# The second norm's first two channel tiles, multiplied before the token root is known

## The chip, the cores and the metric

The kernel runs on one core of one Trainium2 chip. The time is the device time of one execution in microseconds. A core has TensorE (PE in the profile; its weight loads are PEld), VectorE (DVE), ScalarE (ACT), GpSimd (POOL) and SyncE (SP, which here issues DMAs). Each engine takes its own instructions in order and waits at semaphores for the others.

## The reference

One hybrid backbone block over 512 latent tokens of width 2048, with a prefix of 256 context tokens: adaLN norm, two groups of recurrent heads, gates, an output projection with a gated residual, then the part that matters here:

```
x  = x + gt1 * (y @ w_out)
h2 = rmsnorm(x, g_norm2) * (1 + sc2) + sh2        # rmsnorm: x * rsqrt(mean(x*x) + 1e-6) * g, per token
u_gate, u_val = split(h2 @ w_up)                  # 2048 -> 2 x 5504
g  = conv3x3_depthwise(u_gate, 8 x 64 grid) + conv_b
x  = x + gt2 * ((silu(g) * u_val) @ w_down)
return rmsnorm(x, g_final)
```

With s = g_norm2 (1 + sc2) per channel, b = sh2 per channel and r the root per token, a product of h2 with w_up is r * ((s x) @ w_up) + (b @ w_up): the root is one factor for each token, and the shift gives one number for each output channel.

## The kernel before, in words

Activations lie transposed: 16 channel tiles x2[k] of 128 channels (partitions) by 512 tokens. Every matrix product is made in three: an operand is split into a rounded high part and a low part (the remainder), and high by high, high by low and low by high are added in a PSUM bank (`mm3`, L111; its matmuls are recorded at L98). A split is a cast on ScalarE (L90) and a subtraction on VectorE (L91).

The output projection runs in four units wo0 to wo3. Each has four accumulators of 128 channels and goes through the 16 input tiles in eight pairs; a pair loads 128x1024 weights by DMA (`load_split`, tile raw), splits them (hi, lo; two buffers each) and issues 4 x 2 x 3 matmuls of 512 columns. At a unit's end four channel tiles of x2 are updated (L1057) and squared on ScalarE (L1065). The squares of the first twelve tiles are added on VectorE to one tile; the last four tiles' squares stay apart, so five sums are left.

`token_rstd` (L1068) adds each of the five sums over the channels with a matmul by a column of ones: four matmuls of one output column for each, in two passes each, 40 records in all (ps_rms, L1077). A root follows in small steps on ScalarE and VectorE (L159 to L171), and four matmuls spread the root over all partitions (rb_rms, L1088).

The scaling loop (L1137) then goes through the 16 tiles: VectorE multiplies by the root (L84), ScalarE makes the high operand by scale and bias (L1143, tile b), VectorE scales and shifts x2 itself (L1144) and subtracts for the low operand (L81). Tiles 0 to 7 have operands by halves of 256 tokens, tiles 8 to 15 of 512.

`up_two(0)` and `up_two(1)` (L1199) are the first two units of the MLP's up projection, each with four blocks of 128 output channels (two for the gate branch, two for the value branch), eight pairs of channel tiles each; the bank of a gate block is copied to a padded image (L1213), of a value block to val or stage (L1215). Between them `token_sums` builds sums and differences over token halves for a seven-product scheme, which all later blocks (`up_seven`, f = 4 to 42) use, each with its convolution and its share of the down projection. At the end comes a last norm.

A scheduler sets the order of instructions on each engine by priority; `tc.high_priority()` raises it, `tc.keep_in_program_order` pins an instruction to the order in which the code is written, and `tc.issue_after` puts one behind a named other. Tiles come from pools. The pools of the norm (rp among them, which holds the squares and the root) are closed after the root, and the pools fp, tp and bp (the b operands) take their space; the first use of a new tile waits for the last use of what lay there. PSUM has six banks for accumulators and two for small sums.

Of the kernel before, what the change touches and what calls it, by code (L numbers as in the profile page):

```python
# [11 lines left out]
F32 = mybir.dt.float32  # L12
F32R = mybir.dt.float32r
# [5 lines left out]
P = 128  # L19
D = 2048  # L20
# [50 lines left out]
def block_kernel(ctx: ExitStack, tc: tile.TileContext, a: dict, out: bass.AP):  # L71
# [121 lines left out]
    third, turn = [None], [0]  # L193
# [8 lines left out]
    def load_split(src, name, n=2, w=512):  # L202
# [3 lines left out]
        nc.sync.dma_start(raw, src)  # L206
        with tc.high_priority():
            ins = split(hi, lo, raw)
# [862 lines left out]
    def token_rstd(sums, pl, name, n=T, twice=False):  # L1071

        nj = n // P
        ps = psb(f"ps_{name}", (P, nj))
        for i, sq in enumerate(sums):
            for j in range(nj):
                PE.matmul(ps[:, j : j + 1], sq[:, P * j : P * j + P], cst[:, C_ONE : C_ONE + 1],  # L1077
                          start=(i == 0 and j == 0), stop=(i == len(sums) - 1), skip_group_check=True)
        var, scr, r = (pl.tile([P, nj], F32, name=f"{t}_{name}", tag=t) for t in ("rs1", "rs2", "rs3"))
        root(r, ps, D, scr, var)  # L1080
# [6 lines left out]
        for j in range(nj):  # L1087
            PE.matmul(o[:, P * j : P * j + P], r[:, j : j + 1].to_broadcast([P, P]), ident, start=True, stop=True)  # L1088
# [4 lines left out]
    sums2 = []  # L1093
    for n in range(4):
        accs = unit(a["w_out"][n], f"wo{n}", yh, yl)
        with tc.high_priority():
# [4 lines left out]
            for i in range(4):  # L1101
                square(4 * n + i, sums2, rp, "sq")
    with tc.high_priority():
        r2 = token_rstd(sums2, rp, "rms2")
# [30 lines left out]

    with tc.high_priority():
        for k in range(KT):  # L1137
            t = x2[k]
            sk, bk = modc[4][:, k : k + 1], modc[3][:, k : k + 1]
            for sl in (slice(0, TH), slice(TH, T)) if k == 0 else (slice(0, T),):  # L1140
                mul(t[:, sl], t[:, sl], r2[:, sl])
            for sl, (h, l) in halves(k):
                S.activation(h, t[:, sl], AF.Identity, scale=sk, bias=bk)  # L1143
            V.tensor_scalar(out=t, in0=t, scalar1=sk, scalar2=bk, op0=ALU.mult, op1=ALU.add)  # L1144
            for sl, (h, l) in halves(k):
                sub(l, t[:, sl], h.bitcast(F32))
# [31 lines left out]
    stage = [fp.tile([P, T], F32, name=f"stage{i}") for i in range(2)]  # L1178
# [20 lines left out]
    def up_two(n):  # L1199

        accs = [acc(f"u{n}_{i}") for i in range(4)]
        for kp in range(KP):
            wh, wl = load_split(a["w_up0"][n, kp], f"u{n}_{kp}")
            for i, o in enumerate(accs):
                for kk in range(2):
                    k = 2 * kp + kk
                    for sl, (h, l) in halves(k):
                        mm3(o[:, sl], wh[:, kk, P * i : P * i + P], wl[:, kk, P * i : P * i + P],
                            h, l, k == 0 and sl.start == 0, k == KT - 1, skip_group_check=True)
        vals = []  # L1210
        with tc.high_priority():
# [260 lines left out]
```

## Time and profile before

| | |
|---|---|
| median of three runs | 2482.74 us (2481.16 to 2483.55) |
| the profiled execution | 2482.2 us, its span 2480.1 us, mean granted clock 0.993 |
| TensorE busy | 2441.8 us, 98% of the span |
| VectorE, ScalarE, GpSimd busy | 1746.8, 1117.9, 370.4 us |
| output projection's last wide product starts | 1131.64 us |
| first product of the first up unit starts | 1139.15 us |
| first and second up unit end | 1231.97 us |

Rows of the profile give, in this order, a start or a line, the busy time, the engine, the operation with its result and its operands, the shape, and the count of records; a bracket gives the idle time of the engine ahead of the row and what ended it. A matmul's record reaches past the start of the next one, so its cost in a row of equal ones is the distance of the starts. Matmuls with full-precision operands leave two records each.

### The profile page before, as it was taken

What the parts mean: (1) busy time and instruction counts of PE and PEld (TensorE: products, weight loads), DVE (VectorE), ACT (ScalarE), POOL (GpSimd) and SP (SyncE); (2) the same over time, 40 slices, a digit from 0 to 9 for tenths busy, and PEclk for the clock granted to TensorE, in tenths of its full rate; (3) what the DMA queues carried; (4) which work ended last, traced back from release to release, by engine and by line L of the source; (5) the groups of instructions that cost most, each with busy time, mean ns of one, the idle gap of its engine ahead of it and who ended that gap; (6) DMA issues with size and microseconds to landing.
All of it is one profiled execution on the core that took longest, in us unless ns stands there. A gap on an engine that the chain in (4) does not pass through costs nothing.

```text
span 2480.1 us, 35194 instructions
## 1 busy us (share of the span) xinstructions
PE 2441.8 (98%) x13594; PEld 2105.6 (85%) x13594; DVE 1746.8 (70%) x2464; ACT 1117.9 (45%) x1660; POOL 370.4 (15%) x362
## 2 busy tenths in 40 slices
PE   7999999999999999999999999999999999999998
PEld 4888899988988888888888888888888888888887
DVE  5566766554455678867887777777777777777884
ACT  4224544322213444434555555555555555555553
POOL 0000000000000344440011111111111111111101
PEclk9999999999999999999999999999999999999999
DMA  9751112124342778862488888888888888888762
GB/s 374 275 188 52 35 43 77 60 85 136 122 142 94 266 261 297 278 208 95 139 188 192 189 193 190 193 196 191 193 192 189 189 192 189 193 190 190 179 207 68
DMA packets 137911, 429.66 MB, mean 173 GB/s; under 512 B 15504, under 2 KB 19984, under 8 KB 137744
## 3 DMA queue, kind: packets, MB, share of 16 engines
q1 hardware_dynamic: 104688, 348.24, 42.8%
q0 software_dynamic: 31968, 78.66, 20.3%
q8 instruction: 106, 1.74, 0.3%
q10 hardware_dynamic: 1088, 0.52, 0.1%
q14 instruction: 61, 0.50, 0.1%
HBM read 381.22 MB, written 46.14 MB: 172 GB/s over the span
## 4 chain that ended last, share of the span: by engine, by line
PE 91%; issue 3%; DVE 2%; DMA 1%; ACT 0%; POOL 0%; SPq 0%; POOLq 0%; DVEq 0%; ACTq 0%
PE a L98 18%; PE x L98 18%; PE dn L98 16%; PE v L98 9%; PE wo L98 7%; PE ga L98 7%; PE w L98 4%; PE po L98 4%; PE u L98 4%; PE ps_m L98 1%; PE sl L98 1%; PE cst L98 1%; PE s L98 1%; PE mc L325 1%; DMA xl<-in_xT 0%
## 5 line engine op out<-in xcount | busy, mean ns | idle before, releaser
L91 DVE TENSOR_TENSOR lo_q<-q,hi_q 128x1024 fp32r<-128x1024 f32 x195 | 235.4, 1223 | 142.4 <-ACT spare L1323 117.6
L90 ACT CAST hi_q<-q 128x1024 fp32r<-128x1024 f32 x195 | 205.1, 1052 | 229.7 <-PE dn L98 161.9
L98 PE MATMUL dn<-gh,lo_d 128*128 128x512 f32 x660 | 257.2, 390 | 0.0
L98 PE MATMUL dn<-gl,hi_d 128*128 128x512 f32 x660 | 257.2, 390 | 0.0
L98 PE MATMUL dn<-gh,hi_d 128*128 128x512 f32 x660 | 257.1, 390 | 0.0
L1190 DVE SCALAR_TENSOR_TENSOR cv<-pad,cwt,cv 128x512 f32<-128x512 f32 x328 | 246.2, 751 | 6.3 <-ACT cv L1188 0.5
L98 PE MATMUL x<-bt,hi_q 128*128 128x512 f32 x936 | 235.3, 393 | 0.0
L98 PEld LDWEIGHTS x<-bt,hi_q 128*128 128x128 f32 x936 | 167.4, 188 | 30.8
L1231 POOL DMA_DIRECT2D spare<-in_w_up x78 | 68.8, 883 | 731.2 <-DMA spare<-in_w_up 650.2
L314 POOL TENSOR_TENSOR sumg_m<-sumg_m,raw_m 128x512 f32<-128x512 f32 x74 | 124.1, 1677 | 199.4 <-ACT raw_m L313 112.0
L98 PE MATMUL a<-hi_h,hTh 128*128 128x256 f32 x512 | 150.1, 293 | 0.0
L91 DVE TENSOR_TENSOR lo_d<-raw_d,hi_d 128x1024 fp32r<-128x1024 f32 x84 | 101.3, 1206 | 65.9 <-ACT hi_d L90 51.5
L306 DVE SCALAR_TENSOR_TENSOR sum_m<-raw_m,csil,sum_m 128x512 f32<-128x512 f32 x112 | 145.4, 1299 | 1.3
L98 PEld LDWEIGHTS dn<-gl,hi_d 128*128 128x128 f32 x660 | 123.9, 188 | 26.3 <-DVE gl L91 0.2
L98 PEld LDWEIGHTS dn<-gh,hi_d 128*128 128x128 f32 x660 | 123.8, 188 | 26.4 <-ACT gh L90 0.3
L98 PEld LDWEIGHTS dn<-gh,lo_d 128*128 128x128 f32 x660 | 123.9, 188 | 26.2
L98 PE MATMUL a<-lo_h,hTh 128*128 128x256 f32 x512 | 144.7, 283 | 0.0
L98 PE MATMUL a<-hi_h,hTl 128*128 128x256 f32 x512 | 144.7, 283 | 0.0
L91 DVE TENSOR_TENSOR lo_q<-spare,hi_q 128x1024 fp32r<-128x1024 f32 x78 | 95.3, 1222 | 56.7 <-ACT hi_q L90 56.7
L98 PEld LDWEIGHTS x<-bt,lo_q 128*128 128x128 f32 x936 | 125.6, 188 | 10.4 <-ACT u L1297 1.1
L90 ACT CAST hi_h<-raw_h 128x1024 fp32r<-128x1024 f32 x64 | 67.0, 1047 | 138.8 <-PE a L98 131.2
L98 PE MATMUL x<-bt,lo_q 128*128 128x256 f32 x936 | 128.2, 279 | 0.7 <-ACT u L1297 0.7
(366 smaller groups left out, 5864.2 us busy)
## 6 DMA issues: line engine op xcount, KB each, us to landing
raw_m<-in_w_mod SPq DMA_DIRECT2D x192, 512.0 KB, 5.0
q<-in_w_up SPq DMA_DIRECT2D x117, 512.0 KB, 4.5
raw_d<-in_w_down SPq DMA_DIRECT2D x81, 512.0 KB, 3.7
spare<-in_w_up SPq DMA_DIRECT2D x78, 512.0 KB, 4.6
spare<-in_w_up POOLq DMA_DIRECT2D x78, 512.0 KB, 7.4
raw_h<-in_w_heads SPq DMA_DIRECT2D x64, 512.0 KB, 3.5
x2d<-stage POOLq DMA_DIRECT2D x72, 256.0 KB, 5.1
x2d<-spare POOLq DMA_DIRECT2D x72, 256.0 KB, 5.1
```

What stands on the lines that cost most here:

```text
L90: split_ins[0] = S.copy(hi, x).ins
L91: return V.tensor_tensor(out=lo, in0=x, in1=hi.bitcast(F32), op=ALU.subtract).ins
L98: ins = PE.matmul(*args, **kw)
L306: V.scalar_tensor_tensor(out=parts["v"], in0=raw[:, 0, :], scalar=ce, in1=parts["v"], op0=ALU.mult, op1=ALU.add)
L314: G.tensor_tensor(out=parts["g"], in0=parts["g"], in1=raw[:, 1, :], op=ALU.add)
L325: tc.keep_in_program_order(PE.matmul(ps[:, i : i + 1], po[:, P * i : P * i + P], cst[:, C_ONE : C_ONE + 1], start=True, stop=True))
L1190: V.scalar_tensor_tensor(out=t3, in0=src, scalar=w, in1=t3, op0=ALU.mult, op1=ALU.add)
L1231: eng.dma_start(q, a["w_up"][f - FIRST, i, j].rearrange("p k c -> p (k c)"), **kw)
```

## The change

Channel tiles 0 and 1 are multiplied by the norm's scale alone, without the root, and split (unh, unl), while the second output unit still runs. Their products with the first pair of weights of the first up unit (u0_0) go to four accumulators un0 to un3 (`plain_product`), without waiting for the root. TensorE's order is pinned here: blocks 0 and 1, all the sums of squares, block 2, the broadcast, the shift's columns, block 3. The shift's share of these two tiles is a full-precision product of the unsplit weights with the shift column (`shift_column`). VectorE later multiplies the four accumulators by the root (r2s, a copy of the broadcast) into the images and value tiles, and when the unit is done adds its result and the shift's column to them, in place of the four copies. The first up unit starts at its second pair. Tiles 2 and 3 are scaled first and as before; from tile 4 on ScalarE applies scale and bias in place and casts, and VectorE's scale-and-shift falls away. Tiles 0 and 1 are scaled last; the second up unit and the token sums use them. The loads of two pairs are put behind named instructions.

```diff
--- before.py
+++ after.py
@@ -190,7 +190,7 @@
             for f in now:
                 f()
 
-    third, turn = [None], [0]
+    third, turn, last_raw = [None], [0], [None]
 
     def hi_tile(name, n):
 
@@ -204,6 +204,7 @@
         hi = hi_tile(f"hi_{name}", n * w).rearrange("p (n w) -> p n w", n=n)
         lo = wlo.tile([P, n, w], F32R, name=f"lo_{name}", tag="lo")
         nc.sync.dma_start(raw, src)
+        last_raw[0] = raw
         with tc.high_priority():
             ins = split(hi, lo, raw)
         run_later((split_ins[0], ins))
@@ -1068,16 +1069,17 @@
         else:
             add(sums[0], sums[0], sq)
 
-    def token_rstd(sums, pl, name, n=T, twice=False):
+    def token_rstd(sums, pl, name, n=T, twice=False, ps=None, between=lambda: None):
 
         nj = n // P
-        ps = psb(f"ps_{name}", (P, nj))
+        ps = ps or psb(f"ps_{name}", (P, nj))
         for i, sq in enumerate(sums):
             for j in range(nj):
-                PE.matmul(ps[:, j : j + 1], sq[:, P * j : P * j + P], cst[:, C_ONE : C_ONE + 1],
-                          start=(i == 0 and j == 0), stop=(i == len(sums) - 1), skip_group_check=True)
+                mm(ps[:, j : j + 1], sq[:, P * j : P * j + P], cst[:, C_ONE : C_ONE + 1],
+                   start=(i == 0 and j == 0), stop=(i == len(sums) - 1), skip_group_check=True)
         var, scr, r = (pl.tile([P, nj], F32, name=f"{t}_{name}", tag=t) for t in ("rs1", "rs2", "rs3"))
-        root(r, ps, D, scr, var)
+        root(r, ps[:, 0:nj], D, scr, var)
+        between()
         if twice:
             oo = [psb(f"rb_{name}{i}", (P, n)) for i in range(2)]
             for o in oo:
@@ -1085,12 +1087,12 @@
             return oo
         o = psb(f"rb_{name}", (P, n))
         for j in range(nj):
-            PE.matmul(o[:, P * j : P * j + P], r[:, j : j + 1].to_broadcast([P, P]), ident, start=True, stop=True)
+            mm(o[:, P * j : P * j + P], r[:, j : j + 1].to_broadcast([P, P]), ident, start=True, stop=True)
         return o
 
     dr = pool(ctx, "dr", 1, bass.MemoryType.DRAM)
     x2d = [dr.tile([P, T], F32, name=f"x2d{k}", tag=f"x2d{k}") for k in range(KT)]
-    sums2 = []
+    sums2, plain = [], []
     for n in range(4):
         accs = unit(a["w_out"][n], f"wo{n}", yh, yl)
         with tc.high_priority():
@@ -1100,8 +1102,39 @@
                 nc.sync.dma_start(x2d[k], x2[k])
             for i in range(4):
                 square(4 * n + i, sums2, rp, "sq")
+        if n == 2:
+            for k in range(2):
+                plain.append([rp.tile([P, T], F32R, name=f"un{i}{k}") for i in "hl"])
+                h, l = plain[k]
+                S.activation(h, x2[k], AF.Copy, scale=modc[4][:, k : k + 1])
+                V.scalar_tensor_tensor(out=l, in0=x2[k], scalar=modc[4][:, k : k + 1], in1=h.bitcast(F32),
+                                       op0=ALU.mult, op1=ALU.subtract)
+    wh, wl = load_split(a["w_up0"][0, 0], "u0_0")
+    raw0 = last_raw[0]
+    part = [acc(f"un{i}") for i in range(4)]
+    ps = psb("ps_rms2", (P, TJ + 4))
+
+    def plain_product(i):
+
+        c = slice(P * i, P * i + P)
+        for k in range(2):
+            mm3(part[i], wh[:, k, c], wl[:, k, c], *plain[k], k == 0, k == 1)
+
+    def shift_column(i):
+
+        for k in range(2):
+            mm(ps[:, TJ + i : TJ + i + 1], raw0[:, k, P * i : P * i + P], modc[3][:, k : k + 1],
+               start=False, stop=(k == 1), skip_group_check=True)
+
+    pinned[0] = True
     with tc.high_priority():
-        r2 = token_rstd(sums2, rp, "rms2")
+        plain_product(0)
+        plain_product(1)
+        r2 = token_rstd(sums2, rp, "rms2", ps=ps, between=lambda: plain_product(2))
+        for i in range(4):
+            shift_column(i)
+        plain_product(3)
+    pinned[0] = False
     assert not chunks and not later
     st_3.close()
     st_h.close()
@@ -1133,17 +1166,77 @@
             return [(slice(0, T), [b[:, k - KH, :] for b in b1])]
         return [(slice(TH * b, TH * b + TH), [x[:, k, :] for x in b0[b]]) for b in range(2)]
 
+    shift = fp.tile([P, 4], F32, name="shift")
+    stage = [fp.tile([P, T], F32, name=f"stage{i}") for i in range(2)]
+    r2s = tp.tile([P, T], F32, name="r2s", tag="cv")
+    vals0 = [tp.tile([P, T], F32, name="val0", tag="val"), stage[0]]
+
+    def image(x):
+        return x.rearrange("p (r c) -> p r c", c=GW)
+
+    inner = [p[:, 1 : ROWS + 1, 1 : GW + 1] for p in pads]
+    first_parts = [inner[0], image(vals0[0]), inner[1], image(vals0[1])]
+
+    pin = tc.keep_in_program_order
+
+    def columns(k):
+        return modc[4][:, k : k + 1], modc[3][:, k : k + 1]
+
+    def scale(k):
+
+        for sl in (lo, hi) if k == 2 else (slice(0, T),):
+            ins = V.tensor_tensor(out=x2[k][:, sl], in0=x2[k][:, sl], in1=r2[:, sl], op=ALU.mult)
+            pin(ins)
+        return ins
+
+    def lows(k):
+
+        for sl, (h, l) in halves(k):
+            ins = V.tensor_tensor(out=l, in0=x2[k][:, sl], in1=h.bitcast(F32), op=ALU.subtract)
+            pin(ins)
+        return ins
+
+    def unscaled(i):
+        return V.tensor_tensor(out=first_parts[i], in0=image(part[i]), in1=image(r2s), op=ALU.mult)
+
+    lo, hi = slice(0, TH), slice(TH, T)
     with tc.high_priority():
-        for k in range(KT):
-            t = x2[k]
-            sk, bk = modc[4][:, k : k + 1], modc[3][:, k : k + 1]
-            for sl in (slice(0, TH), slice(TH, T)) if k == 0 else (slice(0, T),):
-                mul(t[:, sl], t[:, sl], r2[:, sl])
+        scale(2)
+        scale(3)
+        for k in (2, 3):
+            sk, bk = columns(k)
             for sl, (h, l) in halves(k):
-                S.activation(h, t[:, sl], AF.Identity, scale=sk, bias=bk)
-            V.tensor_scalar(out=t, in0=t, scalar1=sk, scalar2=bk, op0=ALU.mult, op1=ALU.add)
+                pin(S.activation(h, x2[k][:, sl], AF.Identity, scale=sk, bias=bk))
+            pin(V.tensor_scalar(out=x2[k], in0=x2[k], scalar1=sk, scalar2=bk, op0=ALU.mult, op1=ALU.add))
+            lows(k)
+        act_end = S.copy(r2s, r2)
+        pin(act_end)
+        pin(unscaled(0))
+        scale(4)
+        pin(unscaled(1))
+        scaled5 = scale(5)
+        for k in (4, 5):
+            sk, bk = columns(k)
+            pin(S.activation(x2[k], x2[k], AF.Identity, scale=sk, bias=bk))
             for sl, (h, l) in halves(k):
-                sub(l, t[:, sl], h.bitcast(F32))
+                h5 = S.copy(h, x2[k][:, sl])
+                pin(h5)
+        lows(4)
+        dve_end = V.tensor_copy(shift, ps[:, TJ : TJ + 4])
+        pin(dve_end)
+        l5 = lows(5)
+        behind = {(0, 2): (act_end, scaled5), (0, 3): (h5, l5)}
+        for k in (*range(6, KT), 0, 1):
+            mul(x2[k], x2[k], r2)
+            sk, bk = columns(k)
+            S.activation(x2[k], x2[k], AF.Identity, scale=sk, bias=bk)
+            for sl, (h, l) in halves(k):
+                S.copy(h, x2[k][:, sl])
+            for sl, (h, l) in halves(k):
+                sub(l, x2[k][:, sl], h.bitcast(F32))
+            if k in (7, 9):
+                with tc.issue_after(l5.ins):
+                    unscaled(2 + k // 9)
 
     assert not chunks and not later
     lo, hi = slice(0, TH), slice(TH, T)
@@ -1199,15 +1291,25 @@
     def up_two(n):
 
         accs = [acc(f"u{n}_{i}") for i in range(4)]
-        for kp in range(KP):
-            wh, wl = load_split(a["w_up0"][n, kp], f"u{n}_{kp}")
+        k0 = 0 if n else 2
+        for kp in range(k0 // 2, KP):
+            with ExitStack() as order:
+                for ins in behind.get((n, kp), ()):
+                    order.enter_context(tc.issue_after(ins.ins))
+                wh, wl = load_split(a["w_up0"][n, kp], f"u{n}_{kp}")
             for i, o in enumerate(accs):
                 for kk in range(2):
                     k = 2 * kp + kk
                     for sl, (h, l) in halves(k):
                         mm3(o[:, sl], wh[:, kk, P * i : P * i + P], wl[:, kk, P * i : P * i + P],
-                            h, l, k == 0 and sl.start == 0, k == KT - 1, skip_group_check=True)
+                            h, l, k == k0 and sl.start == 0, k == KT - 1, skip_group_check=True)
         vals = []
+        if n == 0:
+            with tc.high_priority():
+                for i, o in enumerate(first_parts):
+                    V.scalar_tensor_tensor(out=o, in0=image(accs[i]), scalar=shift[:, i : i + 1], in1=o,
+                                           op0=ALU.add, op1=ALU.add)
+            return lambda: [conv(i, pads[i], vals0[i]) for i in range(2)]
         with tc.high_priority():
             for i in range(2):
                 S.copy(pads[i][:, 1 : ROWS + 1, 1 : GW + 1], accs[2 * i].rearrange("p (r c) -> p r c", c=GW))
```

Here is what TensorE has at the end of the output projection (wo_3 is its last accumulator, ps_rms the sums, rb_rms the broadcast). Before:

```order
L98 MATMUL wo_3_9152<-yTh_8091,hi_wo_7_9416 128x512
L1077 MATMUL ps_rms_9467<-cst,sqsq_9461 128x1 x4
L98 MATMUL wo_3_9152<-yTl_8092,hi_wo_7_9416 128x512
...
L98 MATMUL wo_3_9152<-yTh_8097,lo_wo_7_9417 128x512
L1077 MATMUL ps_rms_9467<-cst,sqsq_9463 128x1 x4
L1077 MATMUL ps_rms_9467<-cst,sqsq_9465 128x1 x4
L1088 MATMUL rb_rms_9497<-cst,rs_rms_9490 128x128 x4
L98 MATMUL u_0_9616<-b_9526,hi_u_0_9621 128x256
```

And with the change, from the last of block 1 on:

```order
L98 MATMUL un_9482<-unh_9153,lo_u_0_9477 128x512
L98 MATMUL ps_rms_9485<-cst,sqsq_8455 128x1 x4
...
L98 MATMUL ps_rms_9485<-cst,sqsq_9473 128x1 x4
L98 MATMUL un_9483<-unh_9149,hi_u_0_9476 128x512
...
L98 MATMUL un_9483<-unh_9153,lo_u_0_9477 128x512
L98 MATMUL rb_rms_9533<-cst,rs_rms_9520 128x128 x4
L98 MATMUL ps_rms_9485<-mod_63,raw_u_0_9475 128x1 x8
L98 MATMUL un_9484<-unh_9149,hi_u_0_9476 128x512
...
L98 MATMUL un_9484<-unh_9153,lo_u_0_9477 128x512
L98 MATMUL u_0_9675<-b_9576,hi_u_1_9680 128x256
```

The sums, of which three of five stood between wide products, stand in one row behind blocks 0 and 1; block 2 is ahead of the broadcast, the shift and block 3 are behind it.

ScalarE's root and first operands (Activation, DVE, Pool and PE are the engines whose semaphores are waited for; mod_63 is the shift, mod_64 the scale). Before:

```order
L161 ACTIVATE rs_rms_9489<-ps_rms_9467,epsc 128x4 [waits PE_49]
L163 ACTIVATE rs_rms_9490<-rs_rms_9489 128x4 [waits Activation_49]
L1143 ACTIVATE b_9526<-x_0_8011,mod_63,mod_64 128x256 [waits DVE_49,Activation_49,Pool_49]
L1143 ACTIVATE b_9527<-x_0_8011,mod_63,mod_64 128x256 [waits DVE_49]
L1143 ACTIVATE b_9526<-x_1_8017,mod_63,mod_64 128x256 [waits DVE_49]
```

With the change:

```order
L161 ACTIVATE rs_rms_9519<-ps_rms_9485,epsc 128x4 [waits PE_49]
L163 ACTIVATE rs_rms_9520<-rs_rms_9519 128x4 [waits Activation_49]
L1209 ACTIVATE b_9576<-x_2_8023,mod_63,mod_64 128x256 [waits PE_49,DVE_49,Activation_49,Pool_49]
L1209 ACTIVATE b_9577<-x_2_8023,mod_63,mod_64 128x256 [waits DVE_49]
L1209 ACTIVATE b_9576<-x_3_8029,mod_63,mod_64 128x256 [waits DVE_49]
L1209 ACTIVATE b_9577<-x_3_8029,mod_63,mod_64 128x256
L1212 COPY r2s<-rb_rms_9533 128x512
```

The first write of a b operand waits for TensorE as well; in the compiled program the count it waits for is that of the last matmul of block 3, the last reader of the unscaled tiles.

ScalarE near the end of the second up unit (spare is filled by GpSimd's DMA, L1191, with the change L1283, is the SiLU). Before:

```order
L1191 ACT_TABLE_LOAD
L1191 ACTIVATE cv_10057<-cv_10057 128x512
L90 CAST hi_u_5_10339<-raw_u_5_10338 128x1024
L90 CAST gh_10069<-cv_10057 128x512
L1191 ACTIVATE stage_9615<-stage_9615 128x512
L90 CAST hi_u_6_10369<-raw_u_6_10368 128x1024
L90 CAST gh_10084<-stage_9615 128x512
L90 CAST hi_q_3_10525<-spare 128x1024
L90 CAST hi_u_7_10399<-raw_u_7_10398 128x1024
```

With the change:

```order
L90 CAST hi_u_5_10343<-raw_u_5_10342 128x1024
L90 CAST hi_u_6_10373<-raw_u_6_10372 128x1024
L90 CAST hi_q_3_10529<-spare 128x1024
L1283 ACT_TABLE_LOAD
L1283 ACTIVATE cv_10061<-cv_10061 128x512
L1283 ACTIVATE stage_9585<-stage_9585 128x512
L90 CAST hi_u_7_10403<-raw_u_7_10402 128x1024
```

The cast of spare has moved ahead of the table load and both SiLUs, and these stand ahead of the last weights' cast.

1 line of the change is left out of this document (removed).

## The prediction

> **What bounds the kernel now.** I read the page's shares first, then the chain of waits, then TensorE's timeline around the norm, then the stretches with their clock.
>
> ```profile
> PE 2441.8 (98%) x13594; PEld 2105.6 (85%) x13594; DVE 1746.8 (70%) x2464; ACT 1117.9 (45%) x1660; POOL 370.4 (15%) x362
> PE 91%; issue 3%; DVE 2%; DMA 1%; ACT 0%; POOL 0%; SPq 0%; POOLq 0%; DVEq 0%; ACTq 0%
> ```
>
> TensorE bounds the program. No product disappears in this change, so it can win only what TensorE loses around the second norm. TensorE's timeline there (start, us, operation, count of records, and in brackets the idle time ahead of the row and what ended it):
>
> ```profile
> 1117.06 0.39 PE L98 MATMUL wo<-yTh,lo_wo 128*128 128x512 f32 x1
> ...
> 1122.50 0.40 PE L98 MATMUL wo<-yTh,lo_wo 128*128 128x512 f32 x1
> 1122.73 0.28 PE L325 MATMUL mc<-cst,sumg_m 128*128 128x1 f32 x2
> 1122.88 1.03 PE L1077 MATMUL ps_rms<-cst,sqsq 128*128 128x1 f32 x8
> ...
> 1131.87 0.95 PE L1077 MATMUL ps_rms<-cst,sqsq 128*128 128x1 f32 x8
> 1133.55 1.05 PE L1077 MATMUL ps_rms<-cst,sqsq 128*128 128x1 f32 x8 [0.73 <-ACT sqsq L1065]
> 1135.88 2.04 PE L1088 MATMUL rb_rms<-cst,rs_rms 128*128 128x128 f32 x8 [1.27 <-DVE rs_rms L171]
> 1139.15 1.23 PE L98 MATMUL u<-b,hi_u 128*128 128x256 f32 x4 [1.23 <-ACT b L1143]
> 1141.35 0.58 PE L98 MATMUL u<-b,hi_u 128*128 128x256 f32 x1 [0.98 <-DVE b L81]
> ...
> 1145.20 0.28 PE L98 MATMUL u<-b,lo_u 128*128 128x256 f32 x1
> ...
> 1147.91 0.28 PE L98 MATMUL u<-b,hi_u 128*128 128x256 f32 x1
> ```
>
> Four waits: 0.73 for the last square, 1.27 for the root, 1.23 for ScalarE's first operand, 0.98 for VectorE's first low part: 4.2 us. From 1117.06 to 1122.50 lie 24 wide products, so one of 512 columns costs 0.227 us; from 1145.20 to 1147.91 lie 23 of 256 columns, 0.118 each. Then the stretches (us, busy time and count of PE, granted clock, DMA share, GB/s):
>
> ```profile
> 25.44:28.85 3.41, 1.82 (x24) 1.00 1.03 405
> 28.85:35.68 6.83, 4.95 (x11) 0.50 1.05 393
> 496.48:499.89 3.41, 1.68 (x10) 1.00 0.51 154
> 499.89:506.71 6.82, 6.76 (x26) 0.50 0.00 0
> 1127.95:1131.36 3.41, 3.41 (x24) 1.00 0.62 223
> 1131.36:1134.77 3.41, 2.51 (x19) 1.00 0.64 212
> 1134.77:1145.01 10.24, 6.93 (x29) 0.50 0.18 54
> 1145.01:1148.42 3.41, 3.41 (x31) 1.00 0.00 0
> 2459.38:2462.79 3.41, 3.41 (x30) 1.00 0.00 0
> ```
>
> The clock is half from 1134.77 to 1145.01. The three slow stretches last 6.83, 6.82 and 10.24 us: two, two and three times 3.41. Each follows a 3.41-us stretch in which PE was thinly used (1.82, 1.68, 2.51 busy), and of the last one's 2.51 most were sums of one column:
>
> ```profile
> L1077 PE MATMUL ps_rms<-cst,sqsq 128*128 128x1 f32 x16 | 2.0, 246 | 0.7 <-ACT sqsq L1065 0.7
> ```
>
> So the stage loses twice: by waiting, and by the clock that follows.
>
> **What the change removes.** (1) 0.73: the plain products of blocks 0 and 1, 12 x 0.227 = 2.7 us, stand between the last products and the sums; in the row the sums came 1.7 us after the start of the ones ahead. (2) 1.27: the plain product of block 2, 6 x 0.227 = 1.36, covers the root, with 0.1 to spare. (3) The broadcast took 2.04 at half clock; in the program's last norm, at full clock, TensorE's timeline has
>
> ```profile
> 2461.84 0.49 PE L1088 MATMUL rb_rmsf<-cst,rs_rmsf 128*128 128x128 f32 x2
> 2462.53 0.69 PE L1088 MATMUL rb_rmsf<-cst,rs_rmsf 128*128 128x128 f32 x4
> ```
>
> two records in 0.49 and four in 0.69, 0.10 for each more, so eight in 1.1: 0.9 gained (0 if the clock stays half there). (4) The waits 1.23 and 0.98 as they stand go; what comes instead is priced below. (5) The four first u products lay on PE for 1.23; at 0.118 and the tail of one they need about 0.5: 0.7. (6) From 1141.35 to 1145.01, 3.66 us at half clock would be 1.83. (7) The first pair's 48 products of 256 columns, 48 x 0.118 = 5.66, become 24 of 512, 5.44: 0.2. Sum: 0.73 + 1.27 + 0.9 + 2.21 + 0.7 + 1.83 + 0.2 = 7.8 us.
>
> **What it adds on TensorE.** The shift's column is 8 products in full precision, 16 records of one column. The row at 1131.87 has 8 in 0.95, that at 1122.88 8 in 1.03, and a record's own tail is in both; bounds 1.6 and 2.1, I take 1.8. The sums themselves keep their 40 records.
>
> **The new wait.** In the order, ScalarE's first write of a b operand now waits for TensorE too. The b tiles take space that the unscaled tiles of the closed pool held, and the last reader of these is the last plain product of block 3. So no operand of channel tile 2 can be made before that ends (E), though its root has long been there. Behind the waiting write stand all of ScalarE's other casts, the copy of the root, and VectorE's low parts. Rows for the chain:
>
> ```profile
> 1137.95 1.95 DVE L84 TENSOR_TENSOR x<-x,rb_rms 128x256 f32<-128x256 f32 x4 [2.23 <-PE rb_rms L1088]
> 1138.49 4.04 ACT L1143 ACTIVATE b<-x,mod,mod 128x256 fp32r<-128x256 f32 x8 [3.35 <-DVE x L84]
> L84 DVE TENSOR_TENSOR x<-x,rb_rms 128x512 f32<-128x512 f32 x15 | 9.6, 679 | 0.0
> L1143 ACT ACTIVATE b<-x,mod,mod 128x256 fp32r<-128x256 f32 x16 | 8.5, 591 | 8.6 <-DVE x L84 8.6
> L1144 DVE TENSOR_SCALAR x<-x,mod,mod 128x512 f32<-128x512 f32 x16 | 8.3, 541 | 0.0
> L81 DVE TENSOR_TENSOR b<-x,b 128x256 fp32r<-128x256 f32 x16 | 5.9, 417 | 0.0
> L81 DVE TENSOR_TENSOR b<-x,b 128x512 fp32r<-128x512 f32 x8 | 5.3, 684 | 0.0
> ```
>
> VectorE scales tiles 2 and 3 while the shift's records and block 3 run (1.8 + 1.4 = 3.2 us for about 1.9). From E: ScalarE's halves end near E + 0.6 and E + 1.1, VectorE's scale-and-shift of the tile (0.54) near E + 1.7, its first low half (0.42) near E + 2.1. Two products of 0.118 can start in between, so PE idles about 1.9, with the passing of semaphores 2.2. Bounds: 0 if the spaces did not meet (the order excludes it), and above, the old chain from the first b at 1138.49 to the u at 1141.35, 2.86 less the two products, 2.6. I take 2.2, as the chain is nearest to that row.
>
> Without any clock effect: 7.8 - 1.8 - 2.2 = **3.8 us** gained.
>
> **The clock.** Before, sums stood between wide products; now 40 records of one column stand in one row, 40 x 0.11 = 4.4 us, then after 1.4 us of wide products the broadcast (1.0) and the shift (1.8), then 1.4 wide, then the new wait. The stretch ahead of 1134.77 had about 0.7 us of wide products, 2.0 of such records and 0.73 idle, and the clock fell. A 4.4-us row leaves a 3.41-us stretch with at most some 1 us of wide work if it falls within it, and up to 1.7 on each side if not. So I expect a fall. A slow stretch full of products costs half of itself, 1.7 us. One: 3.8 - 1.7 = **2.1 gained**; two: 0.4; three: 1.3 lost.
>
> The Trainium skill, "TensorE: Matmul & The Clock Gate" (Part 1: The HAM clock gate), says that the clock is at full or half rate by a free-running window of 3413 ns in which the unit's activity is watched; its "HAM oscillation" section ties the fall to idle waits that cross a window. The lengths 6.83, 6.82 and 10.24 agree with the window. By the idle rule no fall would come after the change, 3.8 us gained; the row of 1131.36 speaks against it, with 0.73 idle at a stretch and 0.9 in all.
>
> **Costed at nothing, and by what cover.** The unscaled tiles: two casts (0.8 each) and two subtractions (0.75) at the start of the second output unit, where
>
> ```profile
> 995.00 1.22 DVE L91 TENSOR_TENSOR lo_wo<-raw_wo,hi_wo 128x1024 fp32r<-128x1024 f32 x1
> 999.24 1.06 ACT L90 CAST hi_wo<-raw_wo 128x1024 fp32r<-128x1024 f32 x1 [1.74 <-PE wo L98]
> ```
>
> ScalarE itself waits 1.74 for TensorE; without the cover they cost 1.6. The DVE scale-and-shift of tiles 4 to 15 goes to ScalarE: a tile then takes DVE 0.68 + 0.68 and ScalarE about 0.8 + 0.8, while a pair of tiles keeps TensorE for 5.4 us; uncovered, 0.2 a tile. The banks of blocks 0 and 1: PE's first two accumulators give 24 products, 2.8 us, after the low part at E + 2.1; ScalarE's copy of the root and VectorE's multiplication are done near E + 4.1; spare 0.8. The four closing additions (0.74 each) replace four copies.
>
> One place is thin. In ScalarE's order near the end of the second up unit the cast of spare, which waits for a DMA, now stands ahead of the table load, two SiLUs and the last weights:
>
> ```profile
> 1220.73 1.05 ACT L90 CAST hi_q<-spare 128x1024 fp32r<-128x1024 f32 x1 [3.82 <-DMA spare<-in_w_up]
> 1221.68 1.04 ACT L90 CAST hi_u<-raw_u 128x1024 fp32r<-128x1024 f32 x1
> 1214.41 1.93 POOL L1231 DMA_DIRECT2D spare<-in_w_up  x2 [81.06 <-DVE gl L91]
> spare<-in_w_up SPq DMA_DIRECT2D x78, 512.0 KB, 4.6
> spare<-in_w_up POOLq DMA_DIRECT2D x78, 512.0 KB, 7.4
> ```
>
> Cast 1220.73, then load 1.3, SiLUs 1.1, cast 1.05, low part 1.2: about 1226.4. The last pair needs it 24 wide products (5.4 us) ahead of the unit's end, near 1226.5 to 1227: hidden by about 0.5.
>
> **Rivals and chances.** The sum is made against the profiled execution, 2482.2 us (span 2480.1 and 2.1 around it); the median of the three runs is 0.5 above, inside their spread.
>
> A, one slow stretch, 36%: 2482.2 - 2.1 = **2480.1**. For it: plain block 2, then block 3 and the u products are wide enough to restore the clock soon. B, two slow stretches, 27%: 2481.8; the row may straddle a boundary, or the stretch with the shift and the new wait keep the clock down, as the wait rows of 1139.15 and 1141.35 did. C, on the other side, 11%: the clock falls at the 4.4-us row and again in the stretch with broadcast, shift, block 3 and the 2.2 wait, so that three stretches are slow: 2483.5; it decides once more than 3.8 / 1.7 = 2.2 stretches are slow. Against it: 1.4 us of wide products at half clock fill 2.7 of a stretch. D, no fall, 14%: 2478.4. E, the late cast, 6%: with the DMA at 8.6 us in place of 6.3 (1214.41 to 1220.7; queue's median 7.4) 2.3 later less 0.5 cover, 1.8 on A: 2481.9. F, the change doesn't act because the scheduler's order keeps the old waits, or the waits cost more than any row says, 6%: 2482 to 2489.
>
> The range holds A, B, most of C and D, 2477.6 to 2484.0. Two tenths of a per cent, about what a measurement of this kernel can tell from no change, are 5 us: faster lies below 2477.8 and slower above 2487.7. Only D with a shorter new wait gets below: faster 0.13; slower, from C and F with more, 0.05; same 0.82.
>
> **What would show it.** On TensorE: no idle ahead of the sums or the broadcast; an idle of about 2 us after block 3, released by ScalarE's or VectorE's b; the granted clock at 0.50 for one 3.41-us stretch after the sums (A), two (B), three (C) or none (D). On ScalarE: the first b starts as block 3 ends. Idle of TensorE near the end of the second up unit, released by lo_u, would show E. I am wrong if the wait after block 3 is missing or over 3 us, or if TensorE waits for banks in the second pair.

## The result, and the profile after

The change makes the kernel slower: 2494.3 us, the median of five runs, against 2481.6 for the kernel before, measured beside it; the ratio is 1.0054, with a 95% interval of 1.0043 to 1.0064. A sixth run, at a granted clock of 0.715, took 3183.4 us and is not counted. Forecast were 2480.1 us and a range of 2477.6 to 2484.0. The profiled execution took 2491.4 us, the shortest of the five; its span is 2489.4. The busy shares on the changed kernel's profile page:

```profile
PE 2453.3 (99%) x13586; PEld 2109.0 (85%) x13586; DVE 1749.0 (70%) x2461; ACT 1121.4 (45%) x1673; POOL 372.0 (15%) x362
```

TensorE has as much to do as before (8 records fewer) and is busy 11.5 us longer. TensorE's timeline of the changed kernel at the norm:

```profile
1129.15 0.40 PE L98 MATMUL un<-unh,lo_u 128*128 128x512 f32 x1
1129.39 4.52 PE L98 MATMUL ps_rms<-cst,sqsq 128*128 128x1 f32 x40
1133.77 0.48 PE L98 MATMUL un<-unh,hi_u 128*128 128x512 f32 x1
...
1135.59 1.91 PE L98 MATMUL rb_rms<-cst,rs_rms 128*128 128x128 f32 x8
1137.30 2.29 PE L98 MATMUL ps_rms<-mod,raw_u 128*128 128x1 f32 x16
...
1141.93 0.50 PE L98 MATMUL u<-b,hi_u 128*128 128x256 f32 x2 [0.83 <-ACT b L1209]
1143.56 0.39 PE L98 MATMUL u<-b,hi_u 128*128 128x256 f32 x1 [1.13 <-DVE b L1195]
```

Here nearly everything is as forecast. No idle time stands ahead of the sums or the broadcast. The new wait after block 3 is there, 0.83 + 1.13 = 1.96 us (2.2 forecast). The broadcast and the shift's 16 records fall partly into half clock; the shift takes 2.15 us from start to start (1.8 forecast). The clock, in three stretches of its own length:

```profile
1131.41:1134.82 3.41, 3.41 (x28) 1.00 0.15 60
1134.82:1138.23 3.41, 3.41 (x17) 0.50 0.00 0
1138.23:1141.64 3.41, 2.87 (x18) 1.00 0.30 71
```

One stretch at half clock, as in case A, which forecast a gain. So neither the waits nor the clock at the norm explain the loss. Two rows bracket the seven-product blocks, the first product of block 4 and the first sum of the last norm. Before:

```profile
1231.81 0.28 PE L98 MATMUL x<-b,lo_q 128*128 128x256 f32 x1
2451.26 0.83 PE L1077 MATMUL ps_rmsf<-cst,sqfq 128*128 128x1 f32 x6
```

And with the change:

```profile
1229.35 0.40 PE L98 MATMUL x<-b,lo_q 128*128 128x256 f32 x2
2460.60 0.83 PE L98 MATMUL ps_rmsf<-cst,sqfq 128*128 128x1 f32 x6
```

The changed kernel reaches these blocks 2.5 us earlier and leaves them 9.3 us later: 1231.25 us in place of 1219.45, 11.8 more, in code that the change does not touch. No new wait stands there. The 2.5 us are not the norm's gain: the first product of the output projection, ahead of everything that the change does, is as much earlier. Before, and with the change:

```profile
948.41 0.39 PE L98 MATMUL wo<-yTh,hi_wo 128*128 128x512 f32 x1
945.88 0.39 PE L98 MATMUL wo<-yTh,hi_wo 128*128 128x512 f32 x1
```

From there to the first product of block 4 lie 283.4 us before and 283.5 with the change. The stage around the norm gained nothing in this execution.

The groups of TensorE's products in the seven-product blocks (count, busy us, mean ns of one, idle time before), before:

```profile
L98 PE MATMUL dn<-gh,hi_d 128*128 128x512 f32 x660 | 257.1, 390 | 0.0
L98 PE MATMUL x<-bt,lo_q 128*128 128x256 f32 x936 | 128.2, 279 | 0.7 <-ACT u L1297 0.7
L98 PE MATMUL v<-b,hi_q 128*128 128x512 f32 x312 | 77.9, 392 | 0.0
```

and with the change:

```profile
L98 PE MATMUL dn<-gh,hi_d 128*128 128x512 f32 x660 | 256.7, 389 | 0.0
L98 PE MATMUL x<-bt,lo_q 128*128 128x256 f32 x936 | 131.3, 282 | 0.7 <-ACT u L1399 0.7
L98 PE MATMUL v<-b,hi_q 128*128 128x512 f32 x312 | 79.1, 395 | 0.0
```

The same counts, at full clock. Each product of b or bt in these rows takes 3 ns longer, those of the down projection (dn, whose moving operands gh and gl lie in another pool) do not. There are 936 + 4 x 312 = 2,184 products of b and bt with low weights; 3 ns each are 6.6 us, and as many with high weights give most of the rest. Counted from each start to the next, the low weights' products add 6.3 us, the high weights' 4.7 and the down projection's 0.7, which together are all but 0.2 of the 11.8.

The compiled program shows what differs: the tile shift, 16 bytes a partition (32 with its alignment), was created in the pool fp ahead of stage. Everything behind it (stage, p, u, the third high-weight buffer, val, cv, b, bt, spare) lies 32 bytes higher; b starts at byte 96640 of each partition in place of 96608. The weights and yp stay where they were.

### The profile page after: what moved, and what is told of

The parts are those of the page before. It is cut to its first block, busy times and chain, and to the rows that moved or that the text cites. A ratio compares the mean times of both kernels' runs of the same rounds, so it can differ in the third digit from the quotient of the medians.

```text
span 2489.4 us, 35192 instructions
## 1 busy us (share of the span) xinstructions
PE 2453.3 (99%) x13586; PEld 2109.0 (85%) x13586; DVE 1749.0 (70%) x2461; ACT 1121.4 (45%) x1673; POOL 372.0 (15%) x362
## 4 chain that ended last, share of the span: by engine, by line
PE 95%; DVE 2%; DMA 1%; issue 1%; ACT 1%; SPq 0%; DVEq 0%; ACTq 0%; POOLq 0%
PE a L98 18%; PE dn L98 18%; PE x L98 18%; PE v L98 9%; PE ga L98 7%; PE wo L98 7%; PE w L98 4%; PE po L98 4%; PE u L98 3%; PE ps_m L98 1%; PE sl L98 1%; PE dl L98 1%; PE cst L98 1%; PE s L98 1%; PE mc L326 1%
```

## Experiments: where the operands lie

The theory: the place of b and bt in memory sets the price of their products. Its rival: the change's instructions, their order or waits slow the later blocks. First the tile is taken away from the changed kernel.

```diff
-    cbt = fp.tile([P, 152], F32, name="cbt")[:, 0:NF]
+    cbw = fp.tile([P, 152], F32, name="cbt")
+    cbt = cbw[:, 0:NF]
...
-    shift = fp.tile([P, 4], F32, name="shift")
+    shift = cbw[:, 48:52]
```

> The changed kernel with one edit: the shift's column is kept in four unused columns of the tile cbt, so that no tile of its own stands ahead of stage in the pool fp, and every later tile (stage, p, u, the third high buffer, val, cv, b, bt, spare) lies at the address it had before the change, 32 bytes lower. Instructions and their order are unchanged. Theory (addresses): the loss sits in the products with b and bt operands after 1140 us, which take 1 to 4 ns more each in the changed kernel at full clock; it goes away, and what is left is the gain of about 2.4 us at the norm: about 2480 us, 0.999 of before. Rival (the change's instructions, their order or their waits slow the later stages): it stays at 2491 to 2499 us, 1.004 to 1.006 of before.

Measured: 2481.95 us median of ten (2478.4 to 2485.0) beside 2480.92 before, ratio 1.0001 (0.9991 to 1.0011). The whole loss is gone with the 32 bytes. The expected gain of about 2.4 us isn't there; it had taken the 2.5 us from ahead of the output projection for the norm's. The norm follows below.

Then the tile alone is put into the kernel before:

```diff
+    space = fp.tile([P, 4], F32, name="space")
+    V.memset(space, 0.0)
     stage = [fp.tile([P, T], F32, name=f"stage{i}") for i in range(2)]
```

> The kernel before with an unused tile of 16 bytes a partition ahead of stage in the pool fp (written once by a VectorE memset, read by nothing): the same tiles lie 32 bytes higher, as in the changed kernel, and nothing else differs. Theory (addresses): about 12 us slower than before, 2493 us, with TensorE's products of b and bt slower by 1 to 4 ns each. Rival (instructions or their order): no difference, 2482 us.

Measured: 2494.84 us, ratio 1.0056 (1.0041 to 1.0071), as much as the whole change costs. Its groups are those of the changed kernel to the digit:

```profile
L98 PE MATMUL dn<-gh,hi_d 128*128 128x512 f32 x660 | 256.7, 389 | 0.0
L98 PE MATMUL x<-bt,lo_q 128*128 128x256 f32 x936 | 131.3, 282 | 0.7 <-ACT u L1299 0.7
L98 PE MATMUL v<-b,hi_q 128*128 128x512 f32 x312 | 79.1, 395 | 0.0
```

So an unused tile of 16 bytes does it, and the rival falls. What is it about the place? 64 bytes (`[P, 16]` in place of `[P, 4]`):

> As the kernel before with an unused tile, but of 64 bytes a partition, so that the same tiles lie 64 bytes higher. Theory (what counts is the address modulo 64): no difference to before, 2482 us. Rival (any move of these tiles from where they lay, or a larger period): slower, up to 2494 us, or something else than 2482.

Measured: 2490.49 us, 1.0039 (1.0024 to 1.0054): slower too, by less. The remainder modulo 64 is not the rule. Next the 32 bytes stand at the head of the pool bp, so that only b, bt and spare move:

```diff
     bp = pool(st_b, "bp")
+    space = bp.tile([P, 4], F32, name="space")
+    V.memset(space, 0.0)
```

> The kernel before with an unused tile of 16 bytes a partition as the first of the pool bp, so that only b, bt and spare lie 32 bytes higher, while stage, p, u, the third high weight buffer, val and cv stay. Theory (the moving operands of TensorE count): most of the 12 us, 2491 to 2494 us. Rival (the third high buffer, the weights, or VectorE's tiles count): 2482 to 2485 us.

Measured: 2497.39 us, 1.0067 (1.0052 to 1.0082). Moving b and bt alone is enough, and costs more than when the third weight buffer moves along: a sign that it is the distance from the weights that counts. Moving everything tests this:

```diff
-    csil = keep.tile([P, 128], F32, name="csil")[:, 0:KT]
+    csil = keep.tile([P, 136], F32, name="csil")[:, 0:KT]
```

> The kernel before with an unused 32 bytes more in the tile csil of the first pool, so that everything behind it (raw, high and low weights, yp, fp, tp and bp with the b and bt operands) lies 32 bytes higher: the distances between TensorE's moving operands and its weights are those of before, the absolute addresses (modulo 64) those of the changed kernel. Theory (the distance of the moving operand from the weights, or from other tiles, sets the price): no difference, 2480 to 2482 us, and the products of b and bt at the times of before. Rival (the operand's own address modulo 64 or more counts): slower by 7 to 16 us as in the other moved versions, 2488 to 2497 us, perhaps with the output projection's products slower too.

Measured: 2481.75 us, 1.0000 (0.9990 to 1.0009). In this kernel b starts at 96640 as in the changed one, and its groups are those of before:

```profile
L98 PE MATMUL x<-bt,lo_q 128*128 128x256 f32 x936 | 128.2, 279 | 0.7 <-ACT u L1297 0.7
L98 PE MATMUL v<-b,hi_q 128*128 128x512 f32 x312 | 77.9, 392 | 0.0
```

For this move the operands' own addresses count for nothing; a distance counts. Distance to what? One kernel moves the weights and yp against b, one moves yp (x2, gh, gl, and the moving operands of all earlier projections) alone; the tile cbt is cut by 32 bytes in both, so that what lies behind keeps its place. The first reads as follows; in the second the two new lines stand ahead of the pool yp.

```diff
+    space = pool(ctx, "spc").tile([P, 4], F32, name="space")
+    V.memset(space, 0.0)
     whi = pool(ctx, "whi", 2)
...
-    cbt = fp.tile([P, 152], F32, name="cbt")[:, 0:NF]
+    cbt = fp.tile([P, 144], F32, name="cbt")[:, 0:NF]
```

> The kernel before with 32 unused bytes ahead of the weights' pools whi and wlo and the tile cbt cut by 32 bytes, so that the high and low weights and yp (x2, g) lie 32 bytes higher, and pads, stage, the third high buffer, b, bt and spare stay where they were. Theory (the distance between a product's moving operand and its weights sets the price): the products of b and bt with weights in whi and wlo take another time than before, by 1 to 4 ns each (slower is more likely, as in every other moved version, 2484 to 2495 us), those of the down projection, where both moved, do not. Rival (distances within fp, tp and bp, or from b to raw, matter): no change, 2481 us.

> As weights_and_yp_plus32, but the 32 bytes stand behind the weights, so that yp alone moves: the moving operands of the down projection's products (gh, gl), of the output projection's and of the first projections' are 32 bytes further from their weights; b and bt keep their distance. Theory (moving operand to weights): the products of b and bt keep their times to 0.2 ns, those of the down projection and of the output projection change, most likely by 1 to 6 ns each for some 2,000 and 770 of them, 2483 to 2495 us. Rival (distance from b to yp's tiles, which VectorE and ScalarE use meanwhile): the products of b change as in weights_and_yp_plus32.

Measured: 2486.74 us, 1.0021 (1.0012 to 1.0030) with the weights moved, 2505.04 us, 1.0094 (1.0080 to 1.0108) with yp alone. Groups of the first:

```profile
L98 PE MATMUL dn<-gh,hi_d 128*128 128x512 f32 x660 | 257.2, 390 | 0.0
L98 PE MATMUL x<-bt,lo_q 128*128 128x256 f32 x936 | 128.5, 280 | 0.7 <-ACT u L1299 0.7
L98 PE MATMUL v<-b,hi_q 128*128 128x512 f32 x312 | 79.1, 395 | 0.0
```

and of the second:

```profile
L98 PE MATMUL dn<-gh,hi_d 128*128 128x512 f32 x660 | 260.6, 395 | 0.0
L98 PE MATMUL x<-bt,lo_q 128*128 128x256 f32 x936 | 128.3, 279 | 0.7 <-ACT u L1299 0.7
L98 PE MATMUL v<-b,hi_q 128*128 128x512 f32 x312 | 77.9, 392 | 0.0
```

In the first, weights and gh moved together: dn stays at 390, while b's products with high weights rise from 392 to 395. Those of b and bt with low weights moved against their weights too and stay within 1 ns: not every new distance has a price. In the second, gh moved against its weights: dn rises from 390 to 395, the products of b stay. Each time the groups that change are groups whose moving operand and weights moved against each other. In the second the products of the output projection, whose moving operands lie in yp too, rise as well, from a median record of 389 ns to 396.

Two things stay unsettled. The weights of the next product are loaded while one streams (in the changed kernel a product starts at 1225.85 and the next one's load at 1225.86), so the weights that count may be a product's own or those of the next; no run tells them apart. And what stands ahead of a product counts as well: in weights_and_yp_plus32 bt and the third high-weight buffer both stay where they were, and still the products of bt's last tile with the weights in that buffer cost 228.2 ns from start to start in place of 234.0.

By which rule a distance has its price stays open. One guess was tried: the output projection's operands and weights all start at 32 modulo 1024, and its products cost least for their width. Cutting cbt to 72 columns lowers b, bt and the third weight buffer by 320 bytes and gives them this remainder too.

> The kernel before with the tile cbt cut from 152 columns to 72 (43 are used), so that pads, stage, p, u, the third high buffer, val, cv, b, bt and spare lie 320 bytes lower. Then every moving operand and every weight buffer starts at 32 modulo 1024, as the output projection's do, whose products of 512 columns take 226.7 ns, while those of b and bt take 229 to 231 (and 116.6 to 118 for 256 columns, against 113.4 for half of 226.7). Theory (distance 0 modulo 1024 is free of what costs the extra): the products of b and bt fall to 227 and 113.5: 2,183 wide ones less 3 ns and as many half ones less 4, about 15 us faster, 2466 us; at least faster than 2478. Rival (the place in before is the best, and the distance counts in another way): slower, 2485 to 2495 us. Rival (nothing but the distance modulo 64 counts, which is unchanged): 2481 us.

Measured: 2484.71 us, 1.0012 (1.0003 to 1.0021): slower by 3 us, not faster by 15. Between starts, the down projection's products gain 0.4 to 0.9 ns there, and those of b and bt with low weights lose 1.2 to 2.6. The guess is wrong, or not the whole rule.

## Experiments: the norm

With the addresses put back, the change should have gained about 2 us by case A and gained none. The clock's stretches of the profiled execution of shift_in_cbt:

```profile
1133.52:1140.34 6.82, 6.82 (x28) 0.50 0.00 0
1140.34:1143.75 3.41, 3.34 (x23) 1.00 0.17 24
1143.75:1147.17 3.42, 1.54 (x11) 1.00 0.34 132
1147.17:1150.58 3.41, 3.41 (x19) 0.50 0.02 5
```

Two stretches at half clock after the sums, and a third after the one that holds the new wait (busy 1.54 of 3.42): cases A to C are executions of the same instructions, and this one is C. From the first product of the output projection to that of block 4 lie 285.5 us, 2.1 more than before; case C says 1.3 lost, and rival E's waits (0.5 for lo_u, 0.2 for hi_u) make it 2.0. The next kernel takes the wait away: the pool bp is opened so that a tile waits for what lay in its own place.

```diff
-    bp = pool(st_b, "bp")
+    bp = pool(st_b, "bp", waits="tile")
```

> The changed kernel with the shift's column in cbt, as in shift_in_cbt, and the pool bp opened so that a tile waits for the last uses of what lay in its own place, not for the whole pools below: ScalarE's first write of a b operand no longer waits for the last plain product of block 3 (whose unscaled operands lie under bt, which is written much later). Theory (the wait after block 3 is a real cost of about 2 us, on top of which come one to three slow stretches): the 0.8 and 1.1 us of TensorE's idle time ahead of the first u products go, and there is less room for the clock to fall after block 3: 2 to 4 us below shift_in_cbt's 2482, 2478 to 2480 us. Rival (the operands are late for another reason, VectorE's scaling or ScalarE's order): no difference, 2481 to 2482 us.

Measured: 2477.66 us median of eleven, 0.9983 (0.9975 to 0.9992), 4.3 below shift_in_cbt. TensorE's first u product follows block 3 at once:

```profile
1144.31 0.40 PE L98 MATMUL un<-unh,lo_u 128*128 128x512 f32 x1
1144.55 0.50 PE L98 MATMUL u<-b,hi_u 128*128 128x256 f32 x3
```

The wait was the pool's rule and not the data: the unscaled tiles lie under bt and, for 800 bytes, under the end of b1, which are written later. In the profiled execution two stretches at half clock remain, those after the sums:

```profile
1134.61:1141.44 6.83, 6.83 (x28) 0.50 0.00 0
```

Not all of the gain is the wait. From the first product of the output projection to that of block 4 lie 280.3 us, 5.1 less than in shift_in_cbt: 1.96 are the wait, 1.7 the third slow stretch, and about 1.5 are products of the two up units that cost less. Ten us of the first up unit in shift_in_cbt (1151 to 1161) and, in the second row, in this kernel (1150 to 1160):

```profile
L98 PE MATMUL u<-b,hi_u 128*128 128x256 f32 x58 | 10.4, 279 | 0.0
L98 PE MATMUL u<-b,hi_u 128*128 128x256 f32 x61 | 10.5, 276 | 0.0
```

In the compiled programs all operands of these products lie at the same addresses. From start to start a product of 256 columns costs 117.8 ns in both up units of shift_in_cbt and 113.3 in both of this kernel; in two_sums, which comes next, 117.8 in the first and 113.3 in the second. So here the addresses alone do not fix the price. What chooses between the two is not known. The last suspect is the row of sums itself; here three squares more are added on VectorE:

```diff
-        own = k >= KT - (2 if n == 3 * P else 4)
+        own = k >= KT - (1 if n == T else 2 if n == 3 * P else 4)
```

> As bp_waits_by_tile, and the squares of channel tiles 12 to 14 are added on VectorE to the first sum, so that two sums are left in place of five: 8 matmuls of one column (16 records) stand in the row behind blocks 0 and 1 in place of 20 (40 records). Theory (the row of records of one column makes the clock fall): 24 records x 0.11 = 2.6 us less on TensorE, and no slow stretch after it, 1.7 to 3.4 more: 2473 to 2477 us. Rival (the clock falls after any pause of wide products, as broadcast and shift still stand there): 2.6 us less only, 2476 to 2478. Second rival (the added squares come too late and TensorE waits for them): no gain over bp_waits_by_tile.

Measured: 2472.21 us, 0.9963 (0.9950 to 0.9975), 5.4 below the one ahead. TensorE's timeline and, behind it, the clock of this kernel:

```profile
1128.46 0.40 PE L98 MATMUL un<-unh,lo_u 128*128 128x512 f32 x1
1128.93 1.92 PE L98 MATMUL ps_rms<-cst,sqsq 128*128 128x1 f32 x16
1130.70 0.48 PE L98 MATMUL un<-unh,hi_u 128*128 128x512 f32 x1
...
1132.18 1.07 PE L98 MATMUL rb_rms<-cst,rs_rms 128*128 128x128 f32 x8
1133.09 1.84 PE L98 MATMUL ps_rms<-mod,raw_u 128*128 128x1 f32 x16
```

```profile
1127.20:1130.61 3.41, 3.34 (x24) 1.00 0.79 237
1130.61:1134.02 3.41, 3.41 (x27) 1.00 0.14 58
1134.02:1137.43 3.41, 3.41 (x25) 1.00 0.43 100
```

The clock doesn't fall at the norm, the broadcast takes 1.07 in place of 1.91, and the added squares cost next to no waiting (0.07 us idle in the first stretch). This is one execution; over all runs the mean granted clock is 0.995 to 0.997, against 0.993 to 0.996 in bp_waits_by_tile. Of the 5.4, 2.6 are the 24 records; the rest, 2.8, is near the 3.4 of two half-clock stretches less the 0.65 by which the first up unit's products cost more here.

What TensorE still waited for at the end of the second up unit in two_sums, from the list of waits:

```profile
PE u L98 <- ACT hi_u L90: 1.0, 1, 1.0
PE u L98 <- DVE lo_u L91: 0.5, 1, 0.5
```

This is rival E, the last weights behind the cast that waits for a DMA. ScalarE's rows for the two casts:

```profile
1210.10 1.05 ACT L90 CAST hi_q<-spare 128x1024 fp32r<-128x1024 f32 x1 [6.61 <-DMA spare<-in_w_up]
...
1213.52 1.03 ACT L90 CAST hi_u<-raw_u 128x1024 fp32r<-128x1024 f32 x1
```

The last kernel orders that cast behind them (last_split holds the cast of the latest weights):

```diff
     up_two(1)()
+    up_end = last_split[0]
...
-            with tc.high_priority():
+            with tc.high_priority(), ExitStack() as order:
+                if f == FIRST and n == 3:
+                    order.enter_context(tc.issue_after(up_end))
                 split(wh, wl, src)
```

> As two_sums, and in ScalarE's order the cast of spare (which waits for a DMA) is put behind the cast of the second up unit's last weights. Theory (this cast, ahead of the table load, two SiLUs and the last weights, makes TensorE wait at the unit's end): the idle time for hi_u and lo_u there, 1.0 and 0.5 us in two_sums, goes: 2470.5 to 2471 us. Rival (the weights wait for the SiLUs' inputs, or the spare's product is now late itself): no gain over two_sums, 2472 us.

Measured: 2471.05 us, 0.9966 (0.9954 to 0.9978). Both waits are gone from the trace, but in the times it can't be told from two_sums (2472.21, interval 0.9950 to 0.9975): the mechanism is shown, its gain isn't. It and two_sums beat the kernel before by most, 9 to 10 us; bp_waits_by_tile does by 3.7.

## Why the prediction was wrong, point by point

**The step that failed** is the first of all: that the change can act only at the norm ("it can win only what TensorE loses around the second norm") and otherwise only through queues and covers. The sum had no term for where a new tile puts its neighbours. One tile of 16 bytes moved b and bt against their weights, and some 4,400 products pay mostly 1 to 4 ns each: 11.8 us in the blocks from 4 on, and about 1.6 more in the u products of the first two units (120.0 and 233.3 ns from start to start, against 117.8 and 228.9 in shift_in_cbt). Undone alone, the loss goes (shift_in_cbt); done alone, it comes (before_plus32). The diff shows the tile ahead of stage, and the compiled program the addresses. Two marks in the old code should have led there: cbt has 152 columns of which 43 are used, and csil 128 of which 16 are, paddings with no other visible use than to set addresses (csil's, by all_plus32, sets none of the distances here). And the trace of before held a hint: a product of 256 columns cost 0.118 in the up unit, more than half of the 0.227 of one of 512 in the output projection, which I put down to the width.

**What is removed** was right in kind: the waits 0.73 and 1.27 are gone. The sum at the norm was right in size too, once the rest is taken off: case A's 2.1 gained, less 0.5 for rival E's wait and 1.6 for the u products' addresses, is 0.0, and the stage took 283.5 us against 283.4. In shift_in_cbt case C and rival E give 2.0 lost, and 2.1 were. That two such stages agree to 0.1 us is in part luck, as the terms are rounded to 0.1 and more.

**The new wait** was right: its cause (the first b operand waits for block 3's last product) and its size, 1.96 for 2.2. That a per-tile rule removes it without harm wasn't seen; that kernel is 4.3 us faster by the medians, and the wait itself is 1.96 of them.

**The clock**: the forecast that a 4.4-us row of records of one column makes it fall was right, and two_sums shows it by shortening the row to 16. The stretch at 1131.41 is the clearest row: PE busy all of its 3.41 us, and the next one at half. By the rule of the Trainium skill, "TensorE: Matmul & The Clock Gate" (HAM oscillation), idle waits across a window bring the fall; here there was none, so this trace doesn't agree with idleness alone as the cause, while the lengths, 3.41 and 6.82, agree with the window of 3413 ns that the page's Part 1 states. What was mis-sized is the number of stretches. I gave three of them 11%; the changed kernel's profiled execution had one, but that of shift_in_cbt three, and its ten times reach from 2478.4 to 2485.0. The five runs of the changed kernel have mean granted clocks from 0.995 (the shortest, which was profiled) to 0.992 (the longest, 2499.1). So the cases are not rivals of which one holds, they are draws, and that the profile caught case A was luck; the 2.1 us of case A were not there in the median of shift_in_cbt (1.0001). Nor is the loss of before a fixed one: its three half-clock stretches, 10.24 us, were 13.65 in all_plus32, with the same instructions.

**Rival E** held in part: in the changed kernel TensorE waits 0.53 us for lo_u at 1224.12, in two_sums, where the up unit ends earlier, 1.5 for hi_u and lo_u. I had it hidden by 0.5; the DMA was issued at 1210.71 and the cast could start at 1218.35, 7.6 us, between the 6.3 of before and the 8.6 that rival E assumed.

**The chances**: 5% for slower stood on what was worked out at the norm. With a term for addresses as unknown, of either sign and 10 us large, I would have put it near a third, which is a judgement.

## What to carry to other kernels

A new tile is also a change of addresses: compare the compiled placement of every matmul's moving operand and weights before and after, and put small tiles where nothing lies behind them, or in padding that is there. Before an edit of a microsecond is judged by the median, look at the mean time of one product in groups that the edit doesn't touch; if these moved, the edit has not been measured yet. When products are taken ahead of a scale factor as cover, use the cover: shorten the row of thin sums, and let operands wait for their own place rather than for a whole pool.

## What the runs showed of the hardware that was not expected

- The time of a TensorE product at full clock depends on the distance in memory between its moving operand and the weights (its own or the next one's), to 1 to 6 ns of 227: 390 to 395 ns in the record of a dn product with gh 32 bytes further off. Moving both together by 32 bytes changes nothing. Moves of +32, +64 and -320 bytes cost 14, 10 and 3 us over the program by the medians; the remainders tried (64 and 1024) don't explain them.
- The price is steady in the blocks from 4 on: in the profiled executions the six kernels with the distances of before take 1219.45 to 1219.78 us there, the two with those of the changed kernel 1231.08 and 1231.25.
- It is not steady everywhere: at the same addresses the first two up units' products of 256 columns cost 117.8 ns from start to start in shift_in_cbt, 113.3 in bp_waits_by_tile, and in two_sums first the one and then the other.
- The clock falls after 3.41 us in which TensorE was never idle, where the work was records of one column (40 in a row, 4.4 us) for 2.36 us of the stretch and wide products for the rest; the 3.41 us ahead of it, with 2.0 us of such records, brought no fall. With 16 in a row it stayed at 1.00.
